# A two-layer block on one core: two more blocks of the first FFN by seven products, and half a conditioning vector moved into the recurrent mixer

## The chip, the cores and the metric

The kernel runs on one core of one Trainium2 chip. The metric is the device time of one execution in microseconds (us), the median over runs. An execution takes some 1.5 ms, and what is at stake is some us of it.

Five engines work side by side, each with its own order of instructions: PE (TensorE, matrix products), ACT (ScalarE), DVE (VectorE), POOL (GpSimd) and SP (SyncE, which here issues the transfers from device memory). They meet only through semaphores: an instruction waits until what it reads has been written and the place that it writes is free.

## The reference

Two layers, each a mixer and a SwiGLU feed-forward network (FFN). Sequence 512, model width 1024, FFN width 2816, all fp32. A conditioning vector `c` gives six vectors of 1024 per layer, which scale, shift and gate the parts:

```python
cond = jax.nn.silu(c)
h = x
for layer in range(2):
    mod = (cond @ ada_w[layer] + ada_b[layer])[:, None, :]
    sh1, sc1, g1, sh2, sc2, g2 = jnp.split(mod, 6, axis=-1)
    u = rms_norm(h, norm_g[layer, 0]) * (1.0 + sc1) + sh1
    y = hgrn2_mixer(u, ...) if layer == 0 else dilated_attention_mixer(u, ...)
    h = h + (1.0 + g1) * rms_norm(y, norm_g[layer, 1])
    u = rms_norm(h, norm_g[layer, 2]) * (1.0 + sc2) + sh2
    y = swiglu_ffn(u, ffn_w_in[layer], ffn_w_out[layer])
    h = h + (1.0 + g2) * rms_norm(y, norm_g[layer, 3])

def swiglu_ffn(u, w_in, w_out):
    gate, up = jnp.split(u @ w_in, 2, axis=-1)     # w_in: 1024 x 5632
    return (jax.nn.silu(gate) * up) @ w_out
```

`ada_w[layer]` is 1024 x 6144, so the twelve conditioning vectors alone read 48 MB. The six of a layer are numbered v = 0 to 5 in the order of the split (sh1, sc1, g1, sh2, sc2, g2); each is made in two halves hf of 512 columns. Half (l, v, hf) = (1, 1, 0), of which the change speaks, is the first half of sc1 of the second layer, which is read where the attention begins.

## The kernel before

**Products.** An fp32 matrix is split into a high and a low part (`hi`, `lo`, both fp32r), and a product is summed from three: hi by hi, hi by lo, lo by hi. ACT makes the high part of a weight chunk (L90), DVE the low part (L91).

**The stream of weights.** All weights come in one list, `items`, made once (L495 to L569) and worked off in order by the class `Stream`. SP issues the loads into a ring of two buffers `raw` of 1 MB (L61 to L70); a load starts when the buffer two items earlier is free. A `w` item is a weight chunk: L90 and L91 split it into one of three pairs of places. An `ada` item is a chunk of 512 rows and 512 columns of `ada_w`, so a half vector takes two, kq = 0 and 1. What is done with it depends on the vector: for l = 0 and v = 2, 3, 4 (`by_pe`) PE multiplies it (L381, four small products a chunk, which the trace shows as eight) and ACT copies the result; for all others DVE multiplies each of its four slices of 128 rows by a number per row and adds it to `shared` (L401 for the first, L403 for the others). The half vector is then finished: its 128 rows have to be summed. Where `sum_by_pe` holds, PE does it with products by ones (L430, four tiny matmuls, which the trace shows as eight; L448 for a gate); otherwise POOL does it (L405, `partition_all_reduce`), and four DVE instructions pick the diagonal (L415). Two short DVE instructions end it (L419, L421). The order of `w` and `ada` items comes from `weave(ws, others, first, every)`, which puts a group of `others` behind every `every`-th weight.

**The recurrent mixer** (75.6 to 267 us) has eight heads. Per pair of heads three weight chunks are multiplied (`block`, L584 and L586 to L588, 24 products of 128x512 per 128 columns); per head comes a preparation on DVE and POOL (`head_prep`, L1502 to L1543), and four steps `core_a` to `core_d` (L1547 to L1601) of small products on PE: core_a the scores, core_b the states, core_c the output with its normalisation (ACT L1590, DVE L600, POOL L601, DVE L1593), core_d the transposition of the result (L1600). A list of due times (`fl`, L1617 to L1646) puts the steps between the blocks, and a scheduler orders what the engines get. Of the 16 chunks of conditioning vectors in this stage twelve are taken by PE (L381) and four by DVE, woven one group per 0.7 weights.

**The first FFN** begins inside `mixer_out` (L700 to L841) and `ffn` (L999 on), in an order written by hand. The 22 blocks of 128 columns (gate and value each) are done in two ways. PLAIN[0] = 3 pairs of blocks are done plainly: 96 products of 128x512 for two blocks. The other 16 blocks go through `seven_products` (L891 to L997): a block of 2x2 quarters by Strassen's seven products instead of eight, 84 products of 128x256 for a block (L967), for which POOL and DVE add quarters of the weight (L938, L942, L946), ACT and DVE split them (hiq, loq: L954, L958) and DVE sums up. The plain pair j = 1 runs from 340.61 to 362.39 us, the pair j = 2 from 362.39 to 384.15, then the seven products until 536.91 us. While the plain pairs run, ACT, DVE and POOL prepare the first quarters. With PLAIN[1] = 2 the second FFN has the same code with two plain pairs. In the first FFN the two chunks of (1, 1, 0) are woven between the plain pairs' weights and taken by DVE, and POOL sums the half.

Of the kernel before, what the change touches and what calls it, by code (L numbers as in the profile page):

```python
# [301 lines left out]
def block_kernel(tc, x, c, positions, ada_w, ada_b, norm_g, hgrn_w_in, lower, hgrn_norm_g, hgrn_w_out,  # L302
# [8 lines left out]
    with ExitStack() as ctx:  # L311
# [55 lines left out]
            return shared[:, 2 + turns_of_acc[0] % 2]  # L367

        by_pe = lambda l, v, hf: l == 0 and v in (2, 3, 4)
        sum_by_pe = lambda l, v, hf: by_pe(l, v, hf) or (l, v) == (1, 4)  # L370

        def ada_groups(l, v, hf, kq):

# [34 lines left out]
        def ada_item(l, v, hf, kq):  # L408
            src = ada_w[l, kq * 512:(kq + 1) * 512, v * D + hf * 512:v * D + (hf + 1) * 512]
            return ("ada", src.rearrange("(k p) n -> p k n", p=P), ada_chunk(l, v, hf, kq), (l, v, hf, kq))  # L410
# [43 lines left out]
        def fin_item(l, v, hf):  # L454
            if v not in (2, 5):
                return ("do", None, col_fin(l, v, hf), (l, v, hf))
            sl = slice(hf * 512, (hf + 1) * 512)
            b = ada_b[l:l + 1, v * D + hf * 512:v * D + (hf + 1) * 512].broadcast_to((P, 512))
            n = norm_g[l, v // 2 if v == 2 else 3:(2 if v == 2 else 4), sl].broadcast_to((P, 512))
            return ("rows", (b, n), row_fin(l, v, hf), (l, v, hf))  # L460

        def ada_seq(*vecs):

            res, last = [], None
            for l, v in vecs:
                for hf in range(2):
                    res.append([ada_item(l, v, hf, 0)])
                    res.append(([fin_item(*last)] if last else []) + [ada_item(l, v, hf, 1)])
                    last = (l, v, hf)
            return res + [[], [fin_item(*last)]]  # L470

        def ada_halves(l, v):

            return [[ada_item(l, v, hf, kq)] for hf in range(2) for kq in range(2)], [fin_item(l, v, hf) for hf in range(2)]


        def win(w, c0, n=256):
            return ("w", w[:, c0:c0 + n].rearrange("(k p) n -> p k n", p=P))

        def wtok(w, kq, c0):  # L480
            return ("w", w[kq * 512:(kq + 1) * 512, c0:c0 + 512].rearrange("(k p) n -> p k n", p=P))
# [4 lines left out]
        def weave(ws, others, first, every=1):  # L486

            res, o, n = [], list(others), 0
            for i, w in enumerate(ws):
                res.append(w)  # L490
                while i >= first + n * every and o:
                    res += o.pop(0)
                    n += 1
            return res + [i for g in o for i in g]

        items = []
        W = hgrn_w_in[0]
        hg = []
# [4 lines left out]
        hg.append(win(W, 3 * D + 3 * 256))  # L503
        hg_o = [wtok(hgrn_w_out[0], kq, hf * 512) for hf in range(2) for kq in range(2)]

        PLAIN = (3, 2)

        def ffn_ws(l):

            a, w = [], ffn_w_in[l]  # L510
            for j in range(PLAIN[l]):
                a += [win(w, j * 256), win(w, DFF + j * 256)]
            for f in range(2 * PLAIN[l], NF):
                a.append(("quarters", tuple(w[:, c:c + P].rearrange("(k p) n -> p k n", p=P) for c in (DFF + f * P, f * P))))
            return a, [wrow(ffn_w_out[l], j) for j in range(NF // 2)]

        items += weave(hg, ada_seq((0, 2), (0, 4), (0, 3), (1, 4)), 1, 0.7) + hg_o
        f0a, f0b = ffn_ws(0)
        n0 = 2 * PLAIN[0]
        gate, gate_fins = ada_halves(0, 5)  # L520
        one, two = ada_seq((1, 1)), ada_seq((1, 0))
        items += weave(f0a[:n0], [one[0], one[1], [], one[3][:1]], 2) + f0a[n0:]
        late = [gate[0], gate[1], gate[2], gate_fins[:1] + gate[3], one[2], gate_fins[1:] + one[3][1:], two[0], one[5] + two[1]]
        items += weave(f0b, late + two[2:], 0, 0.95)
        AW = attn_w_in[0]

        def av(g, hf):
# [30 lines left out]
        late = ada_seq((1, 2), (1, 3))  # L558
# [469 lines left out]
        def ffn(l, first, close, nxt, side):  # L1028
            turns.close()
            close()  # L1030
            with ExitStack() as fx:
# [4 lines left out]
                with ExitStack() as qx:  # L1036
# [5 lines left out]
                    tl = qp.tile([P, 4, 4, 256], F32R, name=f"tl{l}")  # L1042
                    for j in range(PLAIN[l]):
                        if j == 0:
# [13 lines left out]
                        if j == 0:  # L1058
                            cut()
                            fixed.close()  # L1060
                    seven_products(range(2 * PLAIN[l], NF), mid, pss, spare, th, tl)
                fl.drain()
# [276 lines left out]
        early, late = slice(0, 256), slice(256, S)  # L1339
# [1062 lines left out]
        for kind, g, i in order:  # L2402
            if kind == "v":
                steps += [("v", None, None, k, *p) for k, p in enumerate(value_unit(g - 1, i))]
            else:
                two = sevens(g, i) if by_seven(g) else plain(g, i)
# [120 lines left out]
```

## Time and profile before

| | us |
|---|---|
| median of 3 runs | 1496.64 (1495.39 to 1496.93) |
| the profiled execution, its own time | 1492.7 |
| span in the profile (first to last instruction) | 1491.0 |
| recurrent mixer, first block to the first product of its output matrix | 75.64 to 267.01 |
| first FFN: plain pair j = 2 | 362.39 to 384.15 |
| first FFN: first two blocks by seven products | 384.15 to 403.63 |
| first FFN: the next two | 403.63 to 422.67 |
| second FFN: its last plain pair | 1170.97 to 1192.94 |
| second FFN: its first two blocks by seven products | 1192.94 to 1212.29 |

The granted TensorE clock is 0.999 in the profiled execution. The profiled execution is 3.9 us shorter than the median of the three runs; 1.7 us of its time lie outside the span. In the profile's rows an engine and a line of the code stand first (PE L967), then the operation, what it writes and reads, the shape and the count; PEld is the loading of weights into PE, which runs beside its products. Times in a timeline are from the span's start. Products are pipelined: the time from one start to the next is what each costs, while its own duration is longer.

### The profile page before, as it was taken

What the parts mean: (1) busy time and instruction counts of PE and PEld (TensorE: products, weight loads), DVE (VectorE), ACT (ScalarE), POOL (GpSimd) and SP (SyncE); (2) the same over time, 40 slices, a digit from 0 to 9 for tenths busy, and PEclk for the clock granted to TensorE, in tenths of its full rate; (3) what the DMA queues carried; (4) which work ended last, traced back from release to release, by engine and by line L of the source; (5) the groups of instructions that cost most, each with busy time, mean ns of one, the idle gap of its engine ahead of it and who ended that gap; (6) DMA issues with size and microseconds to landing.
All of it is one profiled execution on the core that took longest, in us unless ns stands there. A gap on an engine that the chain in (4) does not pass through costs nothing. (4 is left out here: it accounts for less than half of the span.)

```text
span 1491.0 us, 25093 instructions
## 1 busy us (share of the span) xinstructions
PE 1467.8 (98%) x9835; PEld 1315.0 (88%) x9835; DVE 1090.9 (73%) x1796; ACT 793.6 (53%) x1470; POOL 191.2 (13%) x172
## 2 busy tenths in 40 slices
PE   8999999999999999999999999999999999999998
PEld 6777788888999988788998999999988899999886
DVE  4587678488688875777798877888776978887533
ACT  4433343373455542257647878567885555555231
POOL 1011112031111100131001010001012211110100
PEclk9999999999999999999999999999999999999999
DMA  9654554115334346644344443354352333334531
GB/s 308 183 175 132 193 170 165 62 59 167 86 114 114 114 149 206 218 141 142 111 118 123 135 121 93 86 163 126 88 199 82 112 88 114 114 114 144 193 116 57
DMA packets 210727, 201.08 MB, mean 135 GB/s; under 512 B 8824, under 2 KB 168496, under 8 KB 210352
## 3 DMA queue, kind: packets, MB, share of 16 engines
q1 hardware_dynamic: 207632, 192.71, 41.5%
q10 hardware_dynamic: 1952, 6.65, 1.2%
q8 instruction: 77, 1.26, 0.3%
q0 software_dynamic: 1024, 0.12, 0.2%
q14 instruction: 42, 0.34, 0.1%
HBM read 192.30 MB, written 5.30 MB: 133 GB/s over the span
## 5 line engine op out<-in xcount | busy, mean ns | idle before, releaser
L90 ACT CAST hi<-raw 128x2048 fp32r<-128x2048 f32 x43 | 82.3, 1913 | 149.3 <-DMA raw<-in_ffn_w_out_dram 78.0
L91 DVE TENSOR_TENSOR lo<-raw,hi 128x2048 fp32r<-128x2048 f32 x43 | 101.8, 2370 | 65.6 <-ACT hi L90 65.6
L586 PE MATMUL ps_mm<-uh,hi 128*128 128x512 f32 (+1 forms) x400 | 145.4, 364 | 0.0
L587 PE MATMUL ps_mm<-ul,hi 128*128 128x512 f32 (+1 forms) x400 | 144.3, 361 | 1.1 <-DVE ul L686 1.1
L588 PE MATMUL ps_mm<-uh,lo 128*128 128x512 f32 (+1 forms) x400 | 143.7, 359 | 0.0
L1988 PE MATMUL ps_mm<-apart,hiq 128*128 128x256 f32 (+1 forms) x608 | 142.3, 327 | 0.3 <-ACT xs L2103 0.2
L1988 PEld LDWEIGHTS ps_mm<-apart,hiq 128*128 128x128 f32 x608 | 99.9, 189 | 8.8 <-ACT xs L2103 0.7
L1988 PE MATMUL ps_mm<-apart,loq 128*128 128x256 f32 (+1 forms) x304 | 97.5, 321 | 0.5 <-DVE loq L2125 0.5
L958 DVE TENSOR_TENSOR loq<-raw,hiq 128x1024 fp32r<-128x1024 f32 x68 | 80.2, 1221 | 22.3 <-ACT hiq L954 22.3
L967 PE MATMUL ps_mm<-th,hiq 128*128 128x256 f32 x340 | 93.8, 276 | 0.0
L967 PE MATMUL ps_mm<-tl,hiq 128*128 128x256 f32 x340 | 93.8, 276 | 0.0
L967 PE MATMUL ps_mm<-th,loq 128*128 128x256 f32 x340 | 93.8, 276 | 0.0
L586 PEld LDWEIGHTS ps_mm<-uh,hi 128*128 128x128 f32 x400 | 75.1, 188 | 18.3 <-issue 6.7
L587 PEld LDWEIGHTS ps_mm<-ul,hi 128*128 128x128 f32 x400 | 75.3, 188 | 12.3 <-DVE ul L686 1.5
L588 PEld LDWEIGHTS ps_mm<-uh,lo 128*128 128x128 f32 x400 | 75.1, 188 | 12.4 <-issue 1.1
L587 PE MATMUL ps_mm<-lo,oh 128*128 128x512 f32 x208 | 81.2, 390 | 3.1 <-DVE lo L91 3.1
L938 POOL TENSOR_TENSOR raw<-raw 128x512 f32<-128x512 f32 x34 | 44.9, 1320 | 301.8 <-DVE loq L934 142.5
L586 PE MATMUL ps_mm<-hi,oh 128*128 128x512 f32 x208 | 81.1, 391 | 0.0
L954 ACT CAST hiq<-raw 128x1024 fp32r<-128x1024 f32 x68 | 68.1, 1047 | 20.8 <-DVE raw L942 19.2
L1988 PE MATMUL ps_mm<-uh,hiq 128*128 128x256 f32 x256 | 71.8, 281 | 0.0
L1988 PE MATMUL ps_mm<-ul,hiq 128*128 128x256 f32 x256 | 71.2, 278 | 0.0
L1988 PE MATMUL ps_mm<-uh,loq 128*128 128x256 f32 x256 | 71.2, 278 | 0.0
(484 smaller groups left out, 4612.9 us busy)
## 6 DMA issues: line engine op xcount, KB each, us to landing
raw<-in_ada_w_dram SPq DMA_DIRECT2D x40, 1024.0 KB, 5.1
raw<-in_ffn_w_in_dram SPq DMA_DIRECT2D x136, 256.0 KB, 4.1
raw<-in_ffn_w_out_dram SPq DMA_DIRECT2D x22, 1024.0 KB, 4.9
raw<-in_attn_w_in_dram SPq DMA_DIRECT2D x64, 256.0 KB, 4.6
raw<-in_hgrn_w_in_dram SPq DMA_DIRECT2D x12, 1024.0 KB, 5.3
raw<-in_attn_w_in_dram SPq DMA_DIRECT2D x12, 1024.0 KB, 5.2
raw<-in_ffn_w_in_dram SPq DMA_DIRECT2D x10, 1024.0 KB, 6.3
raw<-in_attn_w_in_dram SPq DMA_DIRECT2D x16, 512.0 KB, 4.6
```

The source lines that it names most:

```text
L90: self.nc.scalar.copy(hi, t)
L91: self.nc.vector.tensor_sub(lo, t, hi.bitcast(F32))
L586: pe.matmul(ps, ah, bh, start=start, stop=False, skip_group_check=part)
L587: pe.matmul(ps, ah, bl, start=False, stop=False, skip_group_check=part)
L588: pe.matmul(ps, al, bh, start=False, stop=stop, skip_group_check=part)
L938: pool.tensor_add(r[:, 2], r[:, 2], r[:, 0])
L954: act.copy(hi, src)
L958: dve.tensor_sub(lo, src, hi.bitcast(F32))
L967: pe.matmul(ps, w[x][:, a], us[kt][y], start=begin and kt + m == 0, stop=kt == 3 and m == 2, skip_group_check=True)
L1988: pe.matmul(dst(), x, y, start=begin and i == 0, stop=i == len(todo) - 1, skip_group_check=True)
```

## The change

Three edits, all of the code that makes the lists; no instruction's own code is changed.

1. PLAIN becomes (2, 2): the first FFN has two plain pairs and 18 blocks by seven products.
2. Half vector (1, 1, 0) is summed by PE (L430) and no longer by POOL and the diagonal reads.
3. Both chunks of (1, 1, 0) move from the first FFN's stream to the mixer's. There they stand behind the others, and all groups of conditioning chunks are woven one per 0.6 weights instead of one per 0.7, so that they come earlier. The half is finished behind the first chunk of the mixer's output matrix. The first FFN's own weights come with nothing woven in.

```diff
-        sum_by_pe = lambda l, v, hf: by_pe(l, v, hf) or (l, v) == (1, 4)
+        sum_by_pe = lambda l, v, hf: by_pe(l, v, hf) or (l, v) == (1, 4) or (l, v, hf) == (1, 1, 0)
...
-        PLAIN = (3, 2)
+        PLAIN = (2, 2)
...
-        items += weave(hg, ada_seq((0, 2), (0, 4), (0, 3), (1, 4)), 1, 0.7) + hg_o
+        one, two, own = ada_seq((1, 1)), ada_seq((1, 0)), ada_seq((0, 2), (0, 4), (0, 3), (1, 4))
+        items += weave(hg, own[:16] + [one[0], own[17] + one[1]], 1, 0.6) + hg_o[:1] + one[3][:1] + hg_o[1:]
         f0a, f0b = ffn_ws(0)
-        n0 = 2 * PLAIN[0]
         gate, gate_fins = ada_halves(0, 5)
-        one, two = ada_seq((1, 1)), ada_seq((1, 0))
-        items += weave(f0a[:n0], [one[0], one[1], [], one[3][:1]], 2) + f0a[n0:]
         late = [gate[0], gate[1], gate[2], gate_fins[:1] + gate[3], one[2], gate_fins[1:] + one[3][1:], two[0], one[5] + two[1]]
-        items += weave(f0b, late + two[2:], 0, 0.95)
+        items += f0a + weave(f0b, late + two[2:], 0, 0.95)
```

Lines behind L516 have numbers lower by two in the changed kernel (L586 is L584, L1550 is L1548).

The scheduler orders the mixer anew, on all engines; from the entry of the first FFN on the orders of both kernels hold the same rows, but for the pair of blocks and the half vector. Three places show what moves. In the names, `raw` is a buffer of the stream, `cond_tiles` the conditioning input, `uh`, `ul` and `hi`, `lo` the two parts of the mixer's input and of its weights, and a number behind a name tells one buffer's use from the next.

PE before, mixer, two heads' steps one behind the other, with a conditioning chunk at both ends (raw_901, and raw_1027 behind it); the dots are core_c of a head:

```order
L448 MATMUL ps_b_1023<-shared,ones 128x512
L381 MATMUL ps_mm_889<-raw_901,cond_tiles 32x512 x4
L1570 MATMUL ps_b_1078<-v_tok,k_883 128x128 x3
L1550 MATMUL ps_a_1086<-qd_940,ki_941 128x128 x4
L1553 MATMUL ps_a_1086<-qd_940,T_779 32x32 x8
L1556 MATMUL ps_a_1086<-m_964 64x64 x4
L1563 MATMUL ps_a_1105<-ident,k_963 128x128 x3
...
L381 MATMUL ps_mm_1036<-raw_1027,cond_tiles 32x512 x4
L586 MATMUL ps_mm_1050<-uh,hi_790 128x512
```

PE in the changed kernel, the same place; fourteen products of a block stand where the three dots are:

```order
L584 MATMUL ps_mm_984<-uh,hi_719 128x512
L381 MATMUL ps_mm_890<-raw_895,cond_tiles 32x512 x4
L585 MATMUL ps_mm_984<-ul,hi_719 128x512
L586 MATMUL ps_mm_984<-uh,lo_720 128x512
...
L1548 MATMUL ps_a_1013<-qd_861,ki_862 128x128 x4
L1551 MATMUL ps_a_1013<-qd_861,T_750 32x32 x8
L1554 MATMUL ps_a_1013<-m_885 64x64 x4
L1561 MATMUL ps_a_1032<-ident,k_884 128x128 x3
L448 MATMUL ps_b_1044<-shared,ones 128x512
L381 MATMUL ps_mm_1037<-raw_909,cond_tiles 32x512 x4
L584 MATMUL ps_mm_1063<-uh,hi_790 128x512
```

Between one L381 and the next there were before only the two heads' small steps; now a block's products, one core_a and the sum L448 stand there.

PE before, mixer, the transposition L1600 of one head (the dots are nine products, of eleven between L1586 and L430):

```order
L1586 MATMUL ps_b_1255<-state_1161,q_962 128x128
L587 MATMUL ps_mm_1311<-ul,hi_897 128x512
...
L588 MATMUL ps_mm_1311<-uh,lo_898 128x512
L430 MATMUL ps_b_1376<-ones,shared 128x1 x4
L1600 MATMUL ps_a_1339<-ident,aT_1263 128x128 x4
L1550 MATMUL ps_a_1345<-qd_1173,ki_1174 128x128 x4
```

PE in the changed kernel, the same head (the dots are eighteen products, of nineteen between L1584 and L430):

```order
L1584 MATMUL ps_b_1262<-state_1174,q_977 128x128
L586 MATMUL ps_mm_1318<-uh,lo_912 128x512
...
L430 MATMUL ps_b_1376<-ones,shared 128x1 x4
L381 MATMUL ps_mm_1215<-raw_1220,cond_tiles 32x512 x4
L381 MATMUL ps_mm_1390<-raw_1226,cond_tiles 32x512
L1598 MATMUL ps_a_1346<-ident,aT_1270 128x128 x4
L1548 MATMUL ps_a_1352<-qd_1186,ki_1187 128x128 x4
```

More products and a conditioning chunk now stand between the head's output and its transposition.

SP before, the loads of the mixer's last third:

```order
L70 DMA raw_1664<-in_hgrn_w_in_dram 128x8x256
L70 DMA raw_1671<-in_ada_w_dram 128x4x512
L70 DMA raw_1677<-in_hgrn_w_in_dram 128x8x256
L70 DMA raw_1807<-in_ada_w_dram 128x4x512
L70 DMA raw_1813<-in_hgrn_w_in_dram 128x8x256
L70 DMA raw_1938<-in_ada_w_dram 128x4x512
L70 DMA raw_1944<-in_ada_w_dram 128x4x512
L70 DMA raw_2080<-in_ada_w_dram 128x4x512
L70 DMA raw_2086<-in_hgrn_w_out_dram 128x4x512
```

SP in the changed kernel, the same stretch:

```order
L70 DMA raw_1547<-in_hgrn_w_in_dram 128x8x256
L70 DMA raw_1684<-in_ada_w_dram 128x4x512
L70 DMA raw_1690<-in_ada_w_dram 128x4x512
L70 DMA raw_1813<-in_hgrn_w_in_dram 128x8x256
L70 DMA raw_1825<-in_ada_w_dram 128x4x512
L70 DMA raw_1831<-in_ada_w_dram 128x4x512
L70 DMA raw_1956<-in_hgrn_w_in_dram 128x8x256
L70 DMA raw_1969<-in_ada_w_dram 128x4x512
L70 DMA raw_1975<-in_ada_w_dram 128x4x512
L70 DMA raw_2105<-in_hgrn_w_out_dram 128x4x512
```

Two conditioning chunks now come behind each weight chunk, and the last two of them, raw_1969 and raw_1975, are those of (1, 1, 0), taken by DVE.

## The prediction

> **What bounds the kernel now.** I read the page first, then PE's waits, then the stages that the change touches, window by window.
>
> ```profile
> span 1491.0 us, 25093 instructions
> ...
> PE 1467.8 (98%) x9835; PEld 1315.0 (88%) x9835; DVE 1090.9 (73%) x1796; ACT 793.6 (53%) x1470; POOL 191.2 (13%) x172
> ...
> PEclk9999999999999999999999999999999999999999
> ```
>
> PE is busy 98% of the span at full clock. So PE's products count one for one, and work on another engine counts only where PE waits for it. What PE waited for (the last three numbers: us in total, times, longest):
>
> ```profile
> PE ps_mm L587 <- DVE lo L91: 3.1, 2, 2.0
> ...
> PE ps_a L1600 <- DVE aT L1593: 1.6, 1, 1.6
> ...
> PE ps_mm L381 <- DMA raw<-in_ada_w_dram: 0.6, 1, 0.6
> ```
>
> The second and third fall into the recurrent mixer, which the change orders anew. The windows, in this order: the mixer, its last part, the plain pair j = 2, two blocks by seven products, the next two, and the same entry in the second FFN.
>
> ```profile
> core 0: us, PE busy (x) PEld busy (x) DVE busy (x) ACT busy (x) POOL busy (x), PEclk, DMA share, GB/s
> 75.64:267.01 191.37, 189.15 (x1170) 152.03 (x1167) 147.34 (x278) 74.06 (x142) 28.64 (x22) 1.00 0.49 162
> 223.00:267.00 44.00, 44.00 (x280) 37.96 (x279) 37.45 (x64) 17.01 (x31) 8.38 (x6) 1.00 0.43 144
> 362.39:384.15 21.76, 21.76 (x97) 18.02 (x96) 14.33 (x21) 7.86 (x7) 2.73 (x3) 1.00 0.49 133
> 384.15:403.63 19.48, 19.48 (x172) 19.48 (x171) 10.87 (x11) 10.43 (x17) 1.29 (x1) 1.00 0.20 56
> 403.63:422.67 19.04, 19.04 (x170) 19.04 (x169) 15.64 (x16) 11.00 (x19) 2.59 (x2) 1.00 0.39 111
> 1170.97:1192.94 21.97, 21.97 (x100) 18.14 (x98) 20.89 (x19) 8.50 (x10) 3.51 (x2) 1.00 0.33 94
> 1192.94:1212.29 19.35, 19.35 (x172) 19.35 (x171) 10.87 (x11) 10.43 (x17) 1.29 (x1) 1.00 0.21 58
> ```
>
> In the FFN windows PE never waits: these are pure PE time. In the mixer it idles 191.37 - 189.15 = 2.22 us, which are those two waits.
>
> **The pair of blocks.** Removed: the plain pair, 96 products of 128x512 in 21.76 us, 226.7 ns each. Added: two blocks by seven products in the middle of their row, 168 products of 128x256 in 19.04 us, 113.3 ns each. Half the columns cost half the time, so seven products keep their advantage of 7/8: **-2.72 us**. The transfers stay 4 MB for the pair; the DMA share of 0.39 leaves room.
>
> [...]
>
> The entry into the seven products now stands behind pair j = 1. In the second FFN, which has two plain pairs already, the last pair and the first two blocks take 21.97 + 19.35 = 41.32 us; in the first they take 21.76 + 19.48 = 41.24: **+0.08**. Is the first quarter ready, with one plain pair less ahead of it?
>
> ```profile
> 1185.36 2.34 DVE L958 TENSOR_TENSOR loq<-raw,hiq 128x1024 fp32r<-128x1024 f32 x2
> ...
> 1194.59 0.29 PE L967 MATMUL ps_a<-th,hiq 128*128 128x256 f32 x1
> ```
>
> There DVE ends its last low part at 1185.36 + 2.34 = 1187.70, and PE needs it from 1194.59 on: 6.9 us of cover. The order of the changed kernel at the first FFN's entry is that of the second FFN. If the cover failed, the price would be a wait such as the longest one for a low part, quoted below (2.0).
>
> **The half vector.** What leaves the first FFN is eight DVE accumulations, one POOL sum and four diagonal reads.
>
> ```profile
> L403 DVE SCALAR_TENSOR_TENSOR shared<-raw,cond,shared x70: 737/750/1537, 210.7 to 1400.4; 128x512 f32<-128x512 f32 x70
> L405 POOL PARTITION_ALL_REDUCE shared<-shared x8: 3232/3235/3495, 359.3 to 1401.2; - x8
> ```
>
> That is 8 x 0.75 = 6.0 us of DVE and 3.2 of POOL, gone from a stretch where PE waited for neither: worth nothing. In the mixer the 6.0 us come back on DVE, and PE gets one more set of L430. Two rows of such sets, with what follows each:
>
> ```profile
> 203.10 0.95 PE L430 MATMUL ps_b<-ones,shared 128*128 128x1 f32 x8
> 203.98 1.07 PE L381 MATMUL ps_mm<-raw,cond_tiles 128*32 128x512 f32 x8
> ...
> 234.23 0.95 PE L430 MATMUL ps_b<-ones,shared 128*128 128x1 f32 x8
> 235.04 0.48 PE L586 MATMUL ps_mm<-uh,hi 128*128 128x512 f32 x1
> ```
>
> From start to next start 0.88 and 0.81: **+0.85** on the path.
>
> **The mixer's first wait** is for a transfer:
>
> ```profile
> 110.87 1.05 PE L1550 MATMUL ps_a<-qd,ki 128*128 128x128 f32 x8
> ...
> 113.22 1.02 PE L448 MATMUL ps_b<-shared,ones 128*128 128x512 f32 x2
> ...
> 114.17 1.06 PE L381 MATMUL ps_mm<-raw,cond_tiles 128*32 128x512 f32 x8
> ...
> 115.30 0.38 SPq L70 DMA_DIRECT2D raw<-in_ada_w_dram  x1
> ...
> 120.45 1.07 PE L381 MATMUL ps_mm<-raw,cond_tiles 128*32 128x512 f32 x8 [0.65 <-DMA raw<-in_ada_w_dram]
> ```
>
> The chunk at 114.17 frees its buffer, SP issues the next load at 115.30, the data are there at 120.45: 6.28 us behind the first chunk's start. In the new order PE has more between two such chunks: the first chunk itself (1.06), 14 block products (14 x 0.227 = 3.2), a core_a (110.87 to 113.22, 2.35) and L448 (0.95), together 7.6 us. Cover exceeds need by 1.3: the wait of 0.65 goes.
>
> **The second wait** is for a head's output:
>
> ```profile
> 145.66 0.39 PE L1586 MATMUL ps_b<-state,q 128*128 128x128 f32 x2
> ...
> 146.19 1.55 POOL L1542 TENSOR_TENSOR q<-qd,fpre 128x512 f32<-128x512 f32 x1 [7.06 <-PE ps_b L1586]
> ...
> 146.75 1.54 DVE L451 SCALAR_TENSOR_TENSOR gate<-gate,raw 128x512 f32<-128x512 f32 x1
> ...
> 148.42 0.95 PE L430 MATMUL ps_b<-ones,shared 128*128 128x1 f32 x8
> ...
> 149.06 1.02 POOL L601 TENSOR_TENSOR orr<-rv,expo 128x4 f32<-128x4 f32 x1 [1.31 <-DVE fpre L1523]
> 150.10 0.69 DVE L1593 TENSOR_TENSOR aT<-ps_b,orr 128x512 f32<-128x512 f32 x1 [1.06 <-POOL orr L601]
> ...
> 150.94 0.63 PE L1600 MATMUL ps_a<-ident,aT 128*128 128x128 f32 x4 [1.58 <-DVE aT L1593]
> ```
>
> From PE's last L1586 to L1600 the chain over ACT, DVE, POOL and DVE takes 150.94 - 145.66 = 5.28 us (it is held up by DVE's L451, 1.54 long beside POOL's L1542), and PE had eleven products and L430 to fill it. The new order gives it nineteen products (19 x 0.227 = 4.3), L430 (0.88), a chunk (1.06) and a quarter of another (0.27): 6.5 us. Cover exceeds need by 1.2: the wait of 1.58 goes. Together **-2.23**. Both margins are thin, and of the same size as the DVE operations that could slip in.
>
> **New waits.** The mixer's whole order is new, and the old one had two stalls in 191 us. My walk through the new order with these durations finds no certain new one, but margins near 1 us. I bound what may come by zero and by the longest wait for a low part of a weight:
>
> ```profile
> 604.59 0.50 PE L587 MATMUL ps_mm<-lo,oh 128*128 128x512 f32 x1 [1.98 <-DVE lo L91]
> ```
>
> I take **+0.7**, a third of it, nearer zero because the walk finds none. Behind a waiting PE product the whole queue of PE stands, so such a wait counts in full. The mixer's end has slack for its weights:
>
> ```profile
> 250.45 2.29 DVE L91 TENSOR_TENSOR lo<-raw,hi 128x2048 fp32r<-128x2048 f32 x1 [2.76 <-ACT hi L90]
> ...
> 267.01 0.48 PE L586 MATMUL ps_mm<-hi,oh 128*128 128x512 f32 x1
> ```
>
> The output matrix's low part is ready at 252.74 and used at 267.01: 14.3 us, more than the 6.0 us of accumulations and one later load that now stand ahead of it on DVE and on SP.
>
> **Sum:** -2.72 + 0.08 + 0.85 - 2.23 + 0.7 = **-3.3 us**. The profiled execution (span 1491.0, its own time 1492.7) would become 1489.4. It lies 3.9 below the median of the runs shown, 1496.64; put on that, the forecast is **1493.3**. About 0.2%, 3.0 us, is what a measurement of this kernel can tell from no change, so the edge of faster is 1493.65: the forecast is faster while new waits stay under 1.0.
>
> **Rivals.** (A) The stalls only move: a new order trades one late chain for another, since a PE that runs ahead meets the next chain at 5 us with 3.7 us of work. Then only -2.72 + 0.08 + 0.85 = -1.8 remains: 1494.9, no change. For it: margins of 1.2 and 1.3; against: both places have more products now.
>
> (B) Slower: DVE becomes the bound in the mixer's last part. It is busy 37.45 of 44.00 us there, 85%, and its accumulations are twice as long beside a POOL product:
>
> ```profile
> 222.13 3.02 POOL L1539 TENSOR_TENSOR k<-T,fsuf 128x512 f32<-128x512 f32 x1 [29.28 <-DVE ftot L1531]
> ...
> 224.16 1.54 DVE L403 SCALAR_TENSOR_TENSOR shared<-raw,cond,shared 128x512 f32<-128x512 f32 x1
> ```
>
> 1.54 against the usual 0.75. With 6.0 us more, DVE would have 43.5 of 44 us, and the heads' chains (L1593) would queue behind accumulations. If PE waits for all 6.0, the time is 1496.64 - 1.8 + 6.0 = 1500.8; it decides from 1.8 us of new waits on, or from 4.0 if the old ones go too. Against it: the earlier weave spreads the old accumulations forward, and at the end the order puts as many new ones as it takes old ones away.
>
> [...]
>
> (C) The entry into the first FFN's seven products is late, by the 2.0 us of the low part's wait: 1495.3, no change. The second FFN's rows speak against it.
>
> (D) PE's pace is set by weight loads, not columns: PEld is busy 19.04 of 19.04 us in the seven products, 18.02 of 21.76 in the plain pair. By a load-bound pace the plain pair could run at 18.02, and its removal would bring nothing: +1.0 for the swap and 0.85 for L430 with the stalls kept, 1498.6 at most. But its 226.7 ns are measured, so this needs another pace in the place of the pair. [...]
>
> **How the numbers follow.** The forecast's case, old stalls gone and small new ones, 0.64: 0.55 with new waits under 1.0 (faster), 0.09 above (no change). A 0.21, C 0.02, both within 0.2%. B 0.12, slower. D 0.01, between the edges. So faster 0.55; same 0.09 + 0.21 + 0.02 + 0.01 = 0.33; slower 0.12. The range: below, no new wait at all is -4.0, 1492.6, less 1.3, the distance of the lowest run shown from the median: 1491.3. Above, A with one more wait of 1.98 gives 1496.9, and 0.3 for the highest run: 1497.2. That leaves out B in full and little else. The likeliest case's own range is 1491.3 to 1495.0.
>
> **What would show it.** Right: the first FFN's last plain pair and first two seven-product blocks take 41.3 us and the eighteen blocks end 19.0 later than sixteen would; the stretch from the first FFN's entry to the end is 2.6 shorter; the mixer takes 191.37 + 0.85 - 2.23 + 0.7 = 190.7 us; L600 and L1593 no longer appear as releasers of L1600. A shows as a mixer of about 192.2 with PE's idle time again near 2 at other lines; B as DVE above 95% in the last 44 us and PE waiting on DVE lines (lo, aT, shared) there; C as a wait of L967 for loq. The prediction is wrong if the mixer grows by more than 2 us, or if the FFN shrinks by less than 2.

## The result and the profile after

The changed kernel takes 1492.76 us (median of 14 runs, 1490.76 to 1494.96), the kernel before 1496.29 (14 runs, 1495.27 to 1498.14). The ratio is 0.9979, with a 95% interval of 0.9972 to 0.9986: 3.1 us faster, between 2.1 and 4.2. The forecast was 1493.3, faster by 3.3.

One profiled execution does not show this by its span. That of the changed kernel is longer (1492.8) than that of the kernel before (1491.0), and a second profile of each gives 1493.1 and 1495.9. Much of that spread arises ahead of the mixer: in ten of the fourteen profiles of this document the granted clock is below 0.9 between 10 and 20 us, and the mixer begins at 76.7 to 79.6 us; in the other four it is at 1.00 there, and the mixer begins at 75.6 to 76.5. So the stages are compared, not the spans. First the page, as before:

```profile
span 1492.8 us, 25296 instructions
...
PE 1468.0 (98%) x9915; PEld 1318.0 (88%) x9915; DVE 1102.1 (74%) x1800; ACT 799.7 (54%) x1484; POOL 191.0 (13%) x173
```

PE has 80 products more and is busy for the same time. What PE waited for (total, times, longest):

```profile
PE ps_mm L585 <- DVE lo L91: 4.4, 2, 3.2
PE ps_a L2290 <- ACT h L2353: 1.8, 2, 1.4
...
PE ps_mm L381 <- DMA raw<-in_ada_w_dram: 0.6, 1, 0.6
...
PE ps_b L430 <- DVE shared L403: 0.4, 1, 0.4
```

The wait of L1600 (now L1598) is gone. L381 waits for a load as before, but for a later chunk (at 125.80 us). The wait for a low part, which was 1.98 at its longest, is 3.2, and L430 waits, which it did not do before. The windows of the changed kernel: the mixer and what follows it up to the last product of the first FFN's seven products, then the last plain pair and the first two blocks by seven products.

```profile
76.30:268.35 192.05, 190.76 (x1178) 152.96 (x1175) 152.04 (x289) 74.18 (x142) 28.62 (x22) 1.00 0.53 172
268.35:535.42 267.07, 265.79 (x2051) 253.72 (x2050) 200.58 (x230) 144.19 (x259) 41.02 (x35) 1.00 0.34 99
...
341.88:363.87 21.99, 21.99 (x99) 18.17 (x98) 20.93 (x19) 8.88 (x10) 3.51 (x2) 1.00 0.34 95
363.87:383.22 19.35, 19.35 (x172) 19.35 (x170) 10.87 (x11) 10.43 (x17) 1.29 (x1) 1.00 0.20 56
```

And the kernel before from the mixer's end to the same product:

```profile
267.01:536.80 269.79, 268.44 (x1979) 252.68 (x1978) 196.03 (x236) 138.02 (x245) 40.76 (x34) 1.00 0.35 106
```

The first FFN's stretch falls from 269.79 to 267.07, by 2.72; the entry takes 21.99 + 19.35 = 41.34 us without a wait of PE. The mixer, however, reads 192.05 against 191.37: in this execution it did not get shorter at all.

### The profile page after: what moved, and what is told of

It reads as the page before. It is cut to its first block, busy times and chain, and to the rows that moved or that the text cites. A ratio compares the mean times of both kernels' runs of the same rounds, so it can differ in the third digit from the quotient of the medians.

```text
span 1492.8 us, 25296 instructions
## 1 busy us (share of the span) xinstructions
PE 1468.0 (98%) x9915; PEld 1318.0 (88%) x9915; DVE 1102.1 (74%) x1800; ACT 799.7 (54%) x1484; POOL 191.0 (13%) x173
## 3 DMA queue, kind: packets, MB, share of 16 engines
q8 instruction: 78, 1.28, 0.4%
## 5 line engine op out<-in xcount | busy, mean ns | idle before, releaser
L91 DVE TENSOR_TENSOR lo<-raw,hi 128x2048 fp32r<-128x2048 f32 x41 | 97.9, 2391 | 57.8 <-ACT hi L90 57.7
L584 PE MATMUL ps_mm<-uh,hi 128*128 128x512 f32 (+1 forms) x368 | 133.8, 364 | 0.0
L585 PE MATMUL ps_mm<-ul,hi 128*128 128x512 f32 (+1 forms) x368 | 131.2, 356 | 1.1 <-DVE ul L684 1.1
L586 PE MATMUL ps_mm<-uh,lo 128*128 128x512 f32 (+1 forms) x368 | 131.3, 357 | 0.0
L956 DVE TENSOR_TENSOR loq<-raw,hiq 128x1024 fp32r<-128x1024 f32 x72 | 84.9, 1221 | 22.6 <-ACT hiq L952 22.6
L965 PE MATMUL ps_mm<-th,hiq 128*128 128x256 f32 x360 | 99.4, 276 | 0.0
L965 PE MATMUL ps_mm<-tl,hiq 128*128 128x256 f32 x360 | 99.4, 276 | 0.0
L965 PE MATMUL ps_mm<-th,loq 128*128 128x256 f32 x360 | 99.4, 276 | 0.0
L584 PEld LDWEIGHTS ps_mm<-uh,hi 128*128 128x128 f32 x368 | 69.2, 188 | 15.4 <-issue 6.1
L584 PE MATMUL ps_mm<-hi,oh 128*128 128x512 f32 x208 | 81.5, 393 | 0.1
L585 PEld LDWEIGHTS ps_mm<-ul,hi 128*128 128x128 f32 x368 | 69.3, 188 | 11.8 <-DVE ul L684 1.5
L586 PEld LDWEIGHTS ps_mm<-uh,lo 128*128 128x128 f32 x368 | 69.1, 188 | 10.4
```

Source lines behind the costliest of these rows:

```text
L91: self.nc.vector.tensor_sub(lo, t, hi.bitcast(F32))
L584: pe.matmul(ps, ah, bh, start=start, stop=False, skip_group_check=part)
L585: pe.matmul(ps, ah, bl, start=False, stop=False, skip_group_check=part)
L586: pe.matmul(ps, al, bh, start=False, stop=stop, skip_group_check=part)
L956: dve.tensor_sub(lo, src, hi.bitcast(F32))
L965: pe.matmul(ps, w[x][:, a], us[kt][y], start=begin and kt + m == 0, stop=kt == 3 and m == 2, skip_group_check=True)
```

## The experiments

All stages beside each other, in us, from one profile of each kernel (two where two numbers stand). "Stretch" runs from the mixer's end to the last seven-product matmul, "matrix" from there to PE's first transposition for the attention (L667, L665 in the changed kernel), "wait 605" is PE's wait for a low part in the matrix. Ratios are to the kernel before, timed on the same chip.

| kernel | ratio (95%) | mixer | stretch | matrix | wait 605 |
|---|---|---|---|---|---|
| before | 1 | 191.38, 193.11 | 269.78, 269.76 | 115.39, 115.65 | 1.98, 2.09 |
| changed | 0.9979 (0.9972, 0.9986) | 192.05, 191.13 | 267.07, 267.07 | 118.55, 116.25 | 3.17, 2.77 |
| E1 pair only | 1.0072 (1.0053, 1.0091) | 192.82 | 277.59 | 114.61 | 1.04 |
| E2 half vector and weave only | 1.0003 (0.9993, 1.0012) | 191.28 | 269.76 | 115.66 | 2.10 |
| E3 changed, weave 0.7 | 0.9995 (0.9984, 1.0007) | 192.97 | 268.47 | 115.03 | 1.18 |
| E4 changed, POOL sums | 0.9957 (0.9943, 0.9972) | 189.66 | 267.06 | 114.68 | 1.40 |
| E4 again | 0.9944 (0.9929, 0.9959) | 191.12 | 267.06 | 114.88 | 1.37 |
| E5 weave 0.6 only | 0.9977 (0.9967, 0.9986) | 189.50 | 269.78 | 114.60 | 1.04 |
| E7 changed, late chunks sparser | 1.0013 (1.0004, 1.0022) | 191.54 | 267.11 | 120.80 | none |
| E8 changed, PE code shifted | 0.9961 (0.9945, 0.9977) | 191.61 | 267.09 | 114.84 | 1.35 |
| E9 as E4, PE code shifted back | 0.9968 (0.9957, 0.9979) | 190.25 | 267.07 | 117.58 | 2.80 |
| E11 as E1, without the POOL sum | 1.0002 (0.9988, 1.0016) | 191.45 | 269.08 | 114.89 | 1.38 |

**Both kernels again.** No edit.

> The kernel before once more, for a second profile: what a stage differs by here is noise. Theory 'stages are steady': mixer 191.4, mixer's end to last seven-product matmul 269.8, both within 0.3 us; the stretches where PE waits for transfers and low parts (about 10 us and about 605 us) differ by up to 1.5. Rival: the mixer's stalls of 0.65 and 1.58 come and go between executions.

> The changed kernel once more, for a second profile. Theory: mixer 192.0 and first FFN's stretch 267.1 again within 0.3 us, and the 3.2 us wait at 605 us of its first profile is chance, as is the longer tail; the ratio to before is near 0.9979. Rival: the wait at 605 us (a low part of the first FFN's second matrix) is 3.2 again, so it belongs to the change and costs 1.2 us.

Measured: 1.0008 (1.0000 to 1.0017) for the kernel before and 0.9985 (0.9974 to 0.9996) for the changed one. The stretch repeats to 0.02 us. The mixer before does not: 191.38 and 193.11, with the same wait (1.58 and 1.64). The row for 150 to 160 us, where that wait falls, tells why; first the first profile, then the second (columns as in the windows above, the granted clock third from the end):

```profile
150.00:160.00 10.00, 9.06 (x71) 6.54 (x75) 2.90 (x6) 1.17 (x2) 0.07 (x1) 1.00 0.78 263
```

```profile
150.00:160.00 10.00, 8.36 (x63) 6.54 (x63) 3.24 (x9) 1.60 (x3) 1.02 (x1) 0.83 0.65 224
```

In the second the granted clock is 0.83 over those 10 us, which is 1.7 us lost behind a wait of 1.6. Narrower windows show where: the clock is halved for 3.41 us.

```profile
152.07:155.48 3.41, 3.25 (x28) 3.04 (x28) 1.53 (x5) 0.69 (x1) 0.00 (x0) 0.50 0.92 334
```

The same 0.83 stands there in the profiles of E1 and E3, which keep the wait, and 1.00 in E11, which keeps it too: three of five executions with the wait paid for it twice. PE had been idle for 1.49 to 1.78 us in the three, and for 1.58 in the first profile of the kernel before, where the clock stays at 1.00; so what sets the drop off is not shown.

As for the wait near 605 us, the rival held: it is 2.77 in the second profile of the changed kernel, so it belongs to the change. The clock can fall behind this wait too. In the first profile of the changed kernel it did:

```profile
604.42:607.83 3.41, 2.98 (x7) 2.40 (x8) 3.41 (x12) 0.00 (x0) 0.00 (x0) 0.50 0.60 185
```

In the second it stays at 1.00 there, and this is most of what parts that kernel's two numbers for the matrix, 118.55 and 116.25.

**E1, the pair alone.**

```diff
-        PLAIN = (3, 2)
+        PLAIN = (2, 2)
```

> Only PLAIN becomes (2, 2); the half vector (1, 1, 0) stays in the first FFN, summed by POOL, its two chunks now directly ahead of the first quarters. Theory 'the pair is the whole gain' : the stretch from the mixer's end to the last seven-product matmul shrinks by 2.7 us as in the changed kernel, the entry does not wait, and the time is 2.7 below before. Rival 'the move buys the entry': two loads of about 5 us and 6 us of DVE accumulations now stand between the plain weights and the first quarter, whose cover was 6.9 us; PE waits 3 to 9 us at the first L967, and the kernel is between even and 6 us slower than before.

Measured 1.0072 (1.0053 to 1.0091), some 11 us slower (8.4 by the medians, 1503.78 against 1495.43): worse than the rival's 6. The stretch is 277.59, 10.5 us above the changed kernel's, and PE waits there, though not where the rival had it. PE first, then POOL, then DVE:

```profile
370.50 0.38 PE L967 MATMUL ps_mm<-th,hiq 128*128 128x256 f32 x1 [0.82 <-ACT ps_mm L1000]
384.06 0.58 PE L967 MATMUL ps_mm<-uh,hiq 128*128 128x256 f32 x1 [7.83 <-ACT shared L1019]
```

```profile
368.82 3.25 POOL L405 PARTITION_ALL_REDUCE shared<-shared  x1 [6.28 <-DMA raw<-in_ffn_w_in_dram]
379.20 1.25 POOL L938 TENSOR_TENSOR raw<-raw 128x512 f32<-128x512 f32 x1 [7.14 <-issue]
```

```profile
372.10 0.29 DVE L415 CUSTOM_DVE_ANT_0 diag<-shared,ident 128x128 f32<-128x128 f32 x1 [3.80 <-POOL shared L405]
...
372.31 1.75 DVE L934 TENSOR_TENSOR loq<-raw,hiq 128x1536 fp32r<-128x1536 f32 x1
```

The first block waits 0.8 us, the second 7.8, for a quarter whose addition on POOL (L938) starts 7.14 us after the sum ended. For the first 2.0 of these the addition could not start, since it writes the buffer that DVE's L934 reads until 374.06; and L934 itself stood on DVE behind a diagonal read (L415) that waited 3.80 us for the sum. For the other 5.1 us the profile shows nothing that POOL waited for. The two waits make 8.7 of the 10.5 us. Most of the rest is the clock, which is 0.66 from 380 to 390 us.

**E11, the pair alone without that sum.**

```diff
-                if kq == 1 and not sum_by_pe(l, v, hf):
+                if kq == 1 and not sum_by_pe(l, v, hf) and (l, v, hf) != (1, 1, 0):
```

> The kernel with PLAIN (2, 2) alone, in which the sum of half vector (1, 1, 0) by POOL (L405) is left out, so that this half vector is wrong; its loads, accumulations and diagonal reads stay. Theory 'POOL's turn-over is the stall': POOL did nothing for 7.1 us between the sum and the next addition of quarters (L938), and the wait of 7.8 us at the second block of seven products was that; without the sum it falls below 1.5 us, the first FFN's stretch takes 267.1 to 269.0 us, and the kernel is 6.5 to 9 us faster than with the sum, that is 1 to 4 us faster than before. Rival 'loads and accumulations ahead of the quarters are the stall': 5 us or more of the wait stays, and the stretch stays above 274.

```profile
369.77 1.76 DVE L934 TENSOR_TENSOR loq<-raw,hiq 128x1536 fp32r<-128x1536 f32 x1 [1.20 <-ACT hiq L930]
...
371.61 1.29 POOL L938 TENSOR_TENSOR raw<-raw 128x512 f32<-128x512 f32 x1 [9.24 <-DVE cols L421]
...
376.51 0.39 PE L967 MATMUL ps_mm<-uh,hiq 128*128 128x256 f32 x1 [0.74 <-ACT shared L1019]
```

The wait falls from 7.83 to 0.74. The stretch is 8.5 us shorter than E1's, and the kernel 10.5 us faster by the ratios (1.0002 against 1.0072), 7.6 by the medians' distances to the kernel before: the sum on POOL, with what stood behind it, was the stall. E11 takes two things away at once. Counted from the first block's products behind their wait (370.50 and 370.06), the addition starts 7.1 us earlier. Of that 2.1 us are L934, which no longer stands behind a read of the sum, and the other 5 are what is left of POOL's turn-over, the time from the sum's end to POOL's next operation. That the turn-over belongs to the sum, E7 confirms below with 6.97 us, again with no releaser, and in none of the fourteen profiles does POOL's next operation start sooner behind such a sum. What POOL does in these 7 us is not shown.

The kernel isn't faster than before, as the theory had it (by 1 to 4 us; the interval reaches 1.8). The stretch keeps 2.0 us over the changed kernel's 267.07, 1.4 of them in the two waits: the loads and accumulations ahead of the quarters have a price too. So the half vector had to leave this place for the pair to pay in full; whether PE's sum here would have done was not tried.

**E2, the half vector and the weave alone.**

```diff
-        PLAIN = (2, 2)
+        PLAIN = (3, 2)
```

(against the changed kernel, as in all that follow but E5)

> The half vector moves into the mixer with the 0.6 weave and PE's sum, PLAIN stays (3, 2). The prediction's account: the mixer takes 190.7 us (0.7 less than before) and the kernel is 0.7 faster. Rival, from the one profile of the changed kernel: stalls of 2.2 become stalls of 1.3 but PE's own work in the mixer grows by 1.6, the mixer takes 192.0 and the kernel is 0.7 slower than before. Either way the first FFN's stretch keeps its 269.8 us.

Measured 1.0003 (0.9993 to 1.0012): no gain. The mixer takes 191.28, between the two accounts, and the wait near 605 us is that of the kernel before (2.10). From E2 to the changed kernel the pair brings 269.76 - 267.07 = 2.69 us in the stretch.

**E5, the 0.6 weave alone**, from the kernel before:

```diff
-        items += weave(hg, ada_seq((0, 2), (0, 4), (0, 3), (1, 4)), 1, 0.7) + hg_o
+        items += weave(hg, ada_seq((0, 2), (0, 4), (0, 3), (1, 4)), 1, 0.6) + hg_o
```

> The kernel before with the 0.6 weave alone; (1, 1, 0) stays in the first FFN, PLAIN (3, 2). Theory: the two stalls of the mixer (0.65 and 1.58) are gone and no half vector is added, so the mixer takes about 0.7 us less than in the changed kernel (about 190.4) and the kernel is 1 to 2 us faster than before; first FFN's stretch 269.8. Rival: stalls move to the mixer's end, mixer 191.4 or more, no gain.

```profile
76.11:265.61 189.50, 189.50 (x1171) 152.04 (x1167) 147.71 (x279) 74.26 (x142) 29.89 (x22) 1.00 0.50 163
```

PE is busy for all of the mixer's 189.50 us: both stalls are gone, at a price of 0.35 us in PE's own work (189.50 against 189.15). The kernel is 3.4 us faster than before (2.1 to 4.9), as much as the whole change. It was expected at 1 to 2. Not all of it lies in the mixer: the wait near 605 us is 1.04 instead of 1.98 and 2.09, and the matrix is 0.8 to 1.1 shorter, in a stage that the edit does not touch.

**E3, the changed kernel with the old weave.**

```diff
-        items += weave(hg, own[:16] + [one[0], own[17] + one[1]], 1, 0.6) + hg_o[:1] + one[3][:1] + hg_o[1:]
+        items += weave(hg, own[:16] + [one[0], own[17] + one[1]], 1, 0.7) + hg_o[:1] + one[3][:1] + hg_o[1:]
```

> The changed kernel with its conditioning chunks woven one per 0.7 weights, as before; PE's order in the mixer's middle is then that of before. Theory 'the 0.6 weave is what covers the two stalls': PE waits again about 0.7 us at about 121 us (L381) and about 1.5 us at about 152 us (L1598), with more lost where the granted clock drops after the second one; the mixer is at least 1.0 us longer than the 191.1 to 192.1 of the changed kernel. Rival 'the weave does nothing, the move does': no wait at these places, mixer as in the changed kernel. First FFN's stretch 267.1 in both.

```profile
122.20 0.64 PE L381 MATMUL ps_mm<-raw,cond_tiles 128*32 128x512 f32 x4 [0.63 <-DMA raw<-in_ada_w_dram]
...
152.90 0.30 PE L1598 MATMUL ps_a<-ident,aT 128*128 128x128 f32 x1 [1.78 <-DVE aT L1591]
```

Both waits are back, 0.63 us at L381 and 1.78 at L1598, with the clock at 0.83 behind the second; the mixer takes 192.97 (some 1.4 us of its work stand behind the border here, so the stretch reads 268.47). The ratio is 0.9995 (0.9984 to 1.0007). The weave is what covers these two stalls.

**E4, the changed kernel with POOL's sum**, and the same once more.

```diff
-        sum_by_pe = lambda l, v, hf: by_pe(l, v, hf) or (l, v) == (1, 4) or (l, v, hf) == (1, 1, 0)
+        sum_by_pe = lambda l, v, hf: by_pe(l, v, hf) or (l, v) == (1, 4)
```

> The changed kernel with the half vector (1, 1, 0) summed by POOL and the diagonal reads instead of PE. Theory: PE loses one set of L430 (-0.7 to -0.9 us), POOL's sum runs in the mixer's end where PE waits for neither it nor the reads, so the kernel is even to 0.9 us faster than the changed one. Rival: POOL's 3.2 us and the reads stand ahead of DVE and POOL work that the mixer's end or the output matrix's second half waits for, and PE waits 1 to 3 us more there: slower than the changed kernel.

> The changed kernel with POOL's sum once more, beside its shifted copy. Theory: mixer 189.7 without a wait of L430, time 5 to 8 us below the kernel before and 3 to 5 below the changed kernel, as at first. Rival: the first runs were a lucky set; the ratio to before comes out at 0.998 as the changed kernel's.

Measured 1488.38 and 1487.41 us, 0.9957 and 0.9944: 4 to 5 us faster than the changed kernel, far more than the 0.9 expected. The mixer, in the first profile:

```profile
76.47:266.13 189.66, 189.53 (x1170) 152.04 (x1167) 150.73 (x292) 70.90 (x139) 32.84 (x23) 1.00 0.53 174
```

Against the 191.13 and 191.28 of the changed kernel's second profile and E2's, 1.5 us less. The second profile of E4 reads 191.12, against the 189.7 expected: PE waits 0.68 us for a load (L381) and 0.64 at another L430. PE's busy time tells the two sums apart more steadily: 189.53, 189.71 and 189.62 in the profiles of E4, E4 again and E9, with POOL's sum, and 190.68 to 190.78 in those of the changed kernel, E2, E7 and E8, with PE's. Of those 1.1 us 0.9 is the set L430 itself, and its wait for the last accumulation comes on top, here in the changed kernel's second profile:

```profile
252.45 1.05 PE L430 MATMUL ps_b<-ones,shared 128*128 128x1 f32 x8 [0.43 <-DVE shared L403]
```

POOL's sum lies in the mixer's end at 253.7 us, where POOL's next operation comes at 272.3. But the larger part of the gain is elsewhere: the matrix takes 114.68 against 116.25 and 118.55, although no instruction of that stage was touched.

**E8 and E9, PE's code moved by 16 instructions.** E8 takes four filler matmuls out of the head of the changed kernel, E9 adds four to E4 (12 becomes 16). The trace of the changed kernel shows its sixteen fillers (L1343) as 32 products and 32 weight loads, so four are 16 instructions. Here is E8's edit:

```diff
-            busy(12)
+            busy(8)
```

> The changed kernel with four filler matmuls fewer in the head (busy(12) becomes busy(8)); all orders stay the same, but PE's code is 16 instructions shorter from there on, as in the kernel with POOL's sum, so PE's next 16 KB of code is loaded some 2 us later within the first FFN's second matrix. Theory 'code loading decides the wait near 605 us': the code packet no longer falls into the middle of the conditioning load, the load lands in 5.2 us instead of 6.3 to 6.8, the wait falls from 2.8-3.2 to at most 1.6 us, and from the last seven-product matmul to the first L665 it takes 114.7 us as with POOL's sum instead of 116.3 to 118.6; time 1 to 3 us below the changed kernel. Rival 'the place of the sum decides': 116.3 or more again, time as the changed kernel or a little worse for the colder head.

> The kernel with POOL's sum, with four filler matmuls more in the head (busy(12) becomes busy(16)): PE's code has the place that it has in the changed kernel. Theory 'code loading decides': the wait near 605 us is back at 2.8 to 3.2 us and the stretch from the last seven-product matmul to the first L665 at 116.3 or more; time 1.5 to 3.5 above the kernel with POOL's sum, the head up to 1 us of it. Rival 'the place of the sum decides': 114.7 again, time within 1 us of the kernel with POOL's sum.

Both came out by the first theory. E8, with PE's sum, has the short wait (1.35) and 1490.21 us, 2.6 below the changed kernel's median; E9, with POOL's sum, has the long one (2.80) and 1491.09 us, 2.7 to 3.7 above E4. Not all of E9's loss is the wait: its head is 1.7 to 3.1 us longer than E4's (the mixer begins at 79.60 us, against 77.95 and 76.47), and in the matrix, 2.7 to 2.9 us longer, the clock is 0.74 from 600 to 610 us. The chain in the changed kernel (second profile) and then in E8, from the load of a conditioning chunk to PE:

```profile
590.85 0.38 SPq L70 DMA_DIRECT2D raw<-in_ada_w_dram  x1
...
597.10 2.33 DVE L403 SCALAR_TENSOR_TENSOR shared<-raw,cond,shared 128x512 f32<-128x512 f32 x3 [5.08 <-DMA raw<-in_ada_w_dram]
...
600.78 3.23 POOL L405 PARTITION_ALL_REDUCE shared<-shared  x1 [21.06 <-DVE shared L403]
...
601.55 3.62 DVE L91 TENSOR_TENSOR lo<-raw,hi 128x2048 fp32r<-128x2048 f32 x1 [0.86 <-ACT hi L90]
...
605.22 0.50 PE L585 MATMUL ps_mm<-lo,oh 128*128 128x512 f32 x1 [2.77 <-DVE lo L91]
```

```profile
591.18 0.38 SPq L70 DMA_DIRECT2D raw<-in_ada_w_dram  x1
...
596.38 2.33 DVE L403 SCALAR_TENSOR_TENSOR shared<-raw,cond,shared 128x512 f32<-128x512 f32 x3 [4.02 <-DMA raw<-in_ada_w_dram]
...
600.06 3.23 POOL L405 PARTITION_ALL_REDUCE shared<-shared  x1 [20.00 <-DVE shared L403]
...
602.02 2.42 DVE L91 TENSOR_TENSOR lo<-raw,hi 128x2048 fp32r<-128x2048 f32 x1 [2.06 <-ACT hi L90]
...
604.50 0.50 PE L585 MATMUL ps_mm<-lo,oh 128*128 128x512 f32 x1 [1.35 <-DVE lo L91]
```

In the changed kernel the chunk is used 6.25 us after its issue, in E8 5.20. Behind that both chains take the same time. The low part L91 starts 0.8 us after POOL's sum has started and takes 3.62, in E8 it starts 2.0 after it and takes 2.42; but it ends 4.4 us after the sum's start in both. So the load decides: its 1.05 us, and an issue that comes 0.36 us later in the matrix, make the 1.4 us by which the waits differ. In the three profiles with the long use, the changed kernel's two and E9's, it is 6.25 to 6.76 us; in the ten others of the table, E7 left out, it is 5.05 to 5.24. The transfers by queue, in the changed kernel from 590.85 to 597.10 us and in E8 from 591.17 to 596.37:

```profile
q1 hardware_dynamic: 716, 1.82, 81.2%
q8 instruction: 1, 0.02, 1.0%
```

```profile
q1 hardware_dynamic: 610, 1.38, 79.9%
```

A packet of instructions (q8; the changed kernel's profile has 78 with 1.28 MB, 16 KB each) falls into the one load and not into the other; in E8 it comes at 597.1. So it is in the others: in the three profiles with the long use the packet comes 1.4 to 2.6 us after the load's issue, and in the ten with the short one it comes ahead of the issue, or not before the chunk is there. A shift of 16 of PE's instructions moves it, so it is taken to be PE's code. Why a load of 1 MB takes a whole microsecond longer with one such packet in it is not shown: two loads, of 1 MB each, are under way in these windows, and 1.82 MB had been moved when the chunk was used in the changed kernel, 1.38 in E8.

**E7, the late chunks sparser.**

```diff
-        items += f0a + weave(f0b, late + two[2:], 0, 0.95)
+        items += f0a + weave(f0b, late + two[2:], 0, 1.05)
```

> The changed kernel with the first FFN's late conditioning chunks woven one per 1.05 weights of the second matrix instead of one per 0.95, which puts one 1 MB weight chunk ahead of conditioning chunks. Theory 'part of the gain is given back to the stream': the wait of 2.8 to 3.2 us near 605 us (L585 for the low part) shrinks below 1 us, and the kernel is 1 to 2.5 us faster than the changed one unless a later wait takes its place. Rival 'that wait is DVE and POOL colliding, not the load': it stays near 2.8.

```profile
643.07 3.23 POOL L405 PARTITION_ALL_REDUCE shared<-shared  x1 [16.47 <-DVE shared L403]
...
653.28 0.59 POOL L635 TENSOR_TENSOR rr<-rv,expo 128x1 f32<-128x1 f32 x1 [6.97 <-issue]
...
657.86 1.12 PE L665 MATMUL ps_mm<-ident,xn 128*128 128x128 f32 x4 [7.41 <-DVE xn L659]
```

The wait near 605 us went, as expected, but a wait of 7.41 us at the matrix's end took its place, and the kernel is 4.1 us slower than the changed one. The last of POOL's sums, at 635.79 us in E8, comes at 643.07 here, with its chunk, and the matrix's end now meets POOL's turn-over: what L635 reads (rv, L633) is ready at 650.69, but L635 starts at 653.28, 6.97 us behind the sum. The rows that PE waits for hang on it, so that some 2.6 us of the 7.41 are the turn-over's. The wait depends on the loads ahead of it; this is no way to save it.

## Why the prediction came out right

The number was right (1493.3 against 1492.76, a gain of 3.3 against 3.1, 2.1 to 4.2). Step by step:

- **The pair and its entry, -2.72 + 0.08: right.** Measured 269.78 to 267.07 and, from E2, 269.76 to 267.07: -2.7. The rival C did not come: the entry took 41.34 us, as the second FFN's rows had said. D, another pace for products, fell with it.
- **What leaves the first FFN is "worth nothing": true beside three plain pairs only.** With two it would have cost 10.5 us in the stretch (E1 against the changed kernel), 8.5 of them by the sum and what stands behind it (E11). The prediction priced that sum at 3.2 us and did not see the turn-over. The change steps round it, so this did not show in the time.
- **The two old stalls, -2.23: right in mechanism, too small.** E5 and E3 show that the 0.6 weave removes them and the 0.7 weave brings them back. They were worth more than their idle time, since the clock fell behind the second one in three of five executions, at 1.7 us each; E5 gains 3.4 us in all, some 0.8 to 1.1 of it outside of the mixer. The chunk whose margin was put at 1.3 did not make PE wait, but a wait of L381 for a later one came at 0.2 to 0.7 us in four of the nine profiles with the 0.6 weave.
- **PE's sum, +0.85: right as a duration (0.92), too small as a price.** PE's busy time in the mixer grows by 1.1 us with it, and its wait of 0.35 to 0.43 for DVE belongs to it: 1.5 us in all.
- **New waits, +0.7 in the mixer: about right, but one outside of it was missed.** In the mixer they are 1.3 and 0.4 us in the changed kernel's two profiles, L430's for DVE among them. For what follows the first FFN's entry the prediction has no term but the pair's: the orders are the same there but for the pair and the half vector. The wait near 605 us grew by 0.7 to 1.2 us all the same, since PE's code packet now falls into a load (E8, E9), and in one of two profiles the clock fell behind it. Timed, that is 2.6 us between the changed kernel and E8.
- **B, DVE as the bound of the mixer's last part, did not come.** DVE is busy for 39.4 of the mixer's last 44 us (90%) where the rival had 43.5, and PE's only waits there are L430's for DVE, 0.3 and 0.4 us.

So the pair was forecast rightly, and that the total came so close is in part luck: two terms were off and offset each other. The 0.6 weave brought about 3.4 us, where the prediction had 2.2, and moving the half vector with PE's sum took that back (E5 at 0.9977, E2 at 1.0003), where the prediction had 0.85 and 0.7. In the profiles that step costs 1.8 us in the mixer (189.50 to 191.28) and 1.1 in the matrix (114.60 to 115.66); why the matrix grows there is not shown. The pair's 2.7 us are what is left.

One thing stays open. Two profiles of each kernel put the changed one ahead by 0.7 us in the mixer and 2.7 in the stretch and behind by 1.9 in the matrix, together 1.5; the timing says 3.1 (2.1 to 4.2). Of the 1.9 some 0.9 comes from the drop of the clock in one of the two. Profiles with and without a drop of the clock differ by 1.7 us in one stage, so two of each do not settle this.

Better than both kernels is the change with POOL's sum (E4): 1487.4 to 1488.4 us, 0.9944 to 0.9957 of the kernel before. It owes that to the place of PE's code about as much as to the sum: PE's sum with the code shifted (E8) stands at 0.9961, POOL's sum with the code shifted back (E9) at 0.9968.

## What to carry to other kernels

In this case a stall of 1.6 us on TensorE cost twice its idle time where the granted clock fell behind it (0.50 for 3.41 us), so waits of 1.5 us are worth removing, and the cheapest way found here was to hand out side work earlier, not to remove any. Before moving work off GpSimd look at where it stands: the same sum cost some 8 us between two additions (E1 against E11), and TensorE waited for nothing of it where GpSimd had 14.6 us of rest behind it (E4). And before believing a difference of 2 us, move the code by some instructions: a stage that no edit touched took 2.7 to 2.9 us more with 16 instructions more ahead of it (E9 against E4).

## What was not expected of the hardware

- GpSimd's addition after its `PARTITION_ALL_REDUCE` began 7.14 us after the sum's end, with no releaser in the profile (E1), though DVE had freed what it needed 5.1 us before; without the sum the wait behind it fell from 7.83 to 0.74 us (E11). In E7 it was 6.97 us.
- One 16 KB packet of PE's code inside the load of a 1 MB chunk went with 6.3 to 6.8 us from its issue to its use instead of 5.1 to 5.2, and moved with 16 instructions of code (E8, E9).
- The granted clock was halved (0.50) for 3.41 us behind a wait of 1.64 us in the second profile of the kernel before; behind this wait, of 1.49 to 1.78 us, it fell in three of five executions, each time to 0.83 over 10 us.
- A low part of 128x2048 took 3.6 us when it began 0.8 us after the start of GpSimd's sum, 2.4 when it began 2.0 us after it: it ended 4.4 us after the sum's start either way.
